# Folding the pooling's channel maps into the input projection of a two-layer decoder trunk

## The chip, the core and the metric

The kernel runs on one core of one Trainium2 chip. The metric is the device time of one execution in microseconds; the number given for a kernel is the median of its runs. The core has five engines, each with an instruction queue of its own that is worked off in order: TensorE (PE in the profile) multiplies matrices into PSUM; VectorE (DVE) and ScalarE (ACT) work element by element; GpSimd (POOL) does small things here; SyncE (SP) issues all the data transfers (DMA). Engines wait for one another through semaphores.

## What is computed

The input is 2048 tokens of 1024 channels. Two layers follow, each with a residual sum, and a last RMS norm. The change touches the first layer only. There one projection of the normalised tokens gives 512 pooled channels, 512 channels for a state-space model (SSM) and 1024 gate channels. The pooled channels lie in four groups of 128. Group g has a causal mean over the last 2, 4, 8 or 16 tokens, minus the token itself, and then a linear map of its own over its 128 channels:

```
proj = einsum('bsd,de->bse', h, w_in)
u_pool = proj[..., :512]
c = cumsum(u_pool, tokens)                       # per group g, window w
pooled_g = (c - c shifted by w) / min(pos, w) - u_pool_g
mixed_g = einsum('bsc,cd->bsd', pooled_g, pool_w[g])
y_pool = mixed * pool_scale
y = concat([y_pool, y_ssm]) * silu(z)
x = x + einsum('bse,ed->bsd', y, w_out)
```

Sums over tokens and maps over channels can be done in either order.

## The kernel before

**Precision.** Large products run on operands that are split in two parts of type fp32r, a rounded one (`hi`) and the rest (`lo`); a product is the sum of three: hi by hi, hi by lo, lo by hi. Small products (SSM, transposes, norms) run on plain fp32 operands.

**Streams and the planner.** The program is written as many streams (Python generators), each of which yields operations (`Op`), waits for a named event (`Wait`) and requests for buffers (`Alloc`). The class `Sched` merges them when the program is built. It keeps an estimated clock for each engine and a price for each operation, and takes as the next one the operation that can start soonest by these clocks; among those of one engine that can start within a small slack (`SLACK`: 0.02 for PE, 0.3 for SP), the stream of lower rank number goes first, and the stream `main` goes last. The result is one fixed order per engine; on the chip each engine keeps to it and waits where it must. So the prices matter only through the order. The price of a PE batch is in `mmb`:

```
d = sum(width(o) / 2400.0 if x.dtype == F32R else max(width(o), 128 if w.shape[1] > 64 else 0) / 600.0
        for o, w, x, s, e in batch) + 0.0027 * len(batch)
```

By it a fp32r product of 512 columns and a fp32 product of 128 columns have the same price: 0.2133 + 0.0027 = 0.216 us.

**Buffers.** Fixed pools of slots: `st` (8, general), `po` (2, results on their way to DRAM), `raw` (2, weights as loaded), `w` (8, split weights, two for each job), `act` (25), `pwt` (1), and in PSUM `mm` (3 of 1024 columns) and `aux` (2 of 512). A stream that finds no free slot stays behind until one is given back; an `Alloc` of two needs two free at once.

**The main stream** is the list of PE units in fixed order. A unit is one projection of 128 output channels: 8 blocks of input channels, each with 3 products for each block of 512 tokens, so 48 products of 512 columns for 1024 tokens. For the first half of the tokens (A) the order is: `A.s0` to `A.s2` on token block 0, then the same on block 1, `A.s3`, then `A.pu0`, `A.pz0`, `A.pu1`, `A.pz1` and so on to `A.pz3`, then `A.z0` to `A.z3`. `s` are SSM inputs, `pu` the pooled channels of a group, `pz` their gates. The second half (B) runs the same list, then the output projections, then layer 1.

**Weights.** Each unit has a `Job`. `fetch_thread` loads the jobs in their order into the two `raw` slots (512 KB each); `split_thread` makes hi (ACT) and lo (DVE) of them in two `w` slots, which are given back when the unit ends. While the SSM tables are being made, two of the eight `w` slots are taken by them.

**The start.** `norm_block` loads four x tiles of 128 tokens (four `st` slots), scales them (`norm_scale`, ACT, POOL), and once all four are scaled transposes them on PE in 8 steps, each through an `aux` slot to ACT and DVE (`norm_out`). It runs for block 0, then for block 1. The four `st` slots are given back after the last transpose. Beside it `ssm_prep` and what it starts load small tables (15 transfers) and compute the SSM tables, nearly all on DVE. `ssm_tables` makes four tables `ca` of six DVE operations each; for each, `ssm_w` has a batch of 16 small products on PE (the table batches below).

**Pooling.** `post_pool_u` brings the result of a `pu` unit to DRAM (`upd`). `pool_worker` then runs `pool_thread` for the four groups: it loads the tile, makes the window sums and subtracts the token (DVE), loads the group's map `pool_w` (64 KB, through an `st` slot), splits the map and the sums into hi and lo (ACT, DVE), loads the gate `z0d`, multiplies in one batch of six products of 512 columns into an `mm` slot, and scales and gates the result (DVE, from PSUM). The result goes to DRAM and is read much later by the output projection's `ypool_thread`.

Of the kernel before, what the change touches and what calls it, by code (L numbers as in the profile page):

```python
# [70 lines left out]
class Sched:  # L71
    """Merges several instruction streams into one program order. Each stream
    yields its operations; the estimated engine clocks decide which comes next."""
# [15 lines left out]
    def pool(self, name, n, make):  # L89
        """n slots; make(slot, dtype) gives a new tile in a slot."""  # L90
        self.pools[name] = list(range(n))
        self.make[name] = make
# [5 lines left out]
    def done(self, *key):  # L98
        self.keys.add(key)
# [57 lines left out]
    def advance(self, th, value=None):  # L157
        """Runs a stream up to its next operation; True if it got anywhere."""
        moved = False
        if th.block is not None:  # L160
            value = self.unblock(th.block)
            if value is None:
                return False
            th.block = None
            moved = True
        while True:
            try:
                y = th.gen.send(value)
            except StopIteration:
                self.threads.remove(th)  # L170
                return True
            moved = True
            value = None
            if isinstance(y, Op):
                y.ready = self.ready(y)
                th.op = y
                return True
            value = self.unblock(y)
            if value is None:
                th.block = y  # L180
                return True
# [50 lines left out]
def trunk(ctx, tc, io):  # L232
# [24 lines left out]
    slots("pwt", 1, 256)  # L257
# [24 lines left out]
    # ------------------------------------------------------------ operations  # L282
# [58 lines left out]
    def mmb(batch):  # L341
        """A batch of products (out, stationary, moving, start, stop)."""
        d = sum(width(o) / 2400.0 if x.dtype == F32R else max(width(o), 128 if w.shape[1] > 64 else 0) / 600.0
                for o, w, x, s, e in batch) + 0.0027 * len(batch)

        def emit():
            for o, w, x, s, e in batch:
                nc.tensor.matmul(o, w, x, start=s, stop=e)  # L348
        rd = []
        wr = []  # L350
        for o, w, x, s, e in batch:
            for l, ap in ((rd, w), (rd, x), (wr, o)):
                if not any(ap is y for y in l):
                    l.append(ap)
        op = Op("PE", d, rd, wr, emit)
        op.n = len(batch)
        return op
# [9 lines left out]
    # ------------------------------------------------------------ constants  # L367
# [36 lines left out]
    # ------------------------------------------------------------ DRAM scratch  # L404
# [9 lines left out]
    y1d = [[dram(f"y1d{b}_{kp}", (128, 1024)) for kp in range(4)] for b in range(2)]  # L414
    Ed = [dram(f"Ed{u}", (128, 1024)) for u in range(8)]
# [10 lines left out]
    # ------------------------------------------------------------ weights  # L426
    class Job:
        def __init__(self, srcs, name):
            self.srcs, self.name, self.pool = srcs, name, "w"
# [4 lines left out]
    def job_cols(w, c0, name):  # L434
        return Job([(lambda r: r.rearrange("p (k e) -> p k e", k=NK),
                     w[:, c0:c0 + 128].rearrange("(k p) e -> p k e", p=128))], name)

# [12 lines left out]
    def fetch_thread():  # L450
        for job in jobs:
            job.raw = yield Alloc("raw")
            for view, src in job.srcs:
                yield dma(view(job.raw), src)
            done("raw", job)
# [12 lines left out]
    # ------------------------------------------------------------ activations  # L468
    class Acts:
        """hi/lo parts of a [channels, 1024 tokens] operand: slots of two k by 512 tokens."""  # L470
# [46 lines left out]
    # ------------------------------------------------------------ rms norm  # L517
# [10 lines left out]
    def norm_block(src, keys, gname, acts, b, gate=None):  # L528
        """Normalises 512 tokens and puts them into acts, channels on partitions."""
        if gate:  # L530
            yield Wait(gate)
        xs = []
        for t in range(4):
            yield Wait(keys(b * 4 + t))
            if src is None:
                x = x1t.pop(keys(b * 4 + t)[1:])
            else:
                x = yield Alloc("st")
                yield dma(x[:, :1024], src(b * 4 + t))
            xs.append(x)  # L540
            boot = acts is h0[0] and b == 0
            spawn(norm_scale(xs[t][:, :1024], (acts.name, "n", b, t), boot), 1 if boot else 2, f"{acts.name}n{b}{t}")
        done("boot", acts.name, b)
        for t in range(4):
            yield Wait((acts.name, "n", b, t))
        yield Wait(("vcol",))
        for k in range(NK):
            if k % 2 == 0:
                yield from acts.alloc(k // 2, b)
            ps = yield Alloc("aux")  # L550
            yield trb([(ps[:, t * 128:(t + 1) * 128], xs[t][:, k * 128:(k + 1) * 128], ident) for t in range(4)])
            spawn(norm_out(ps, gname, acts, k, b), 1, f"{acts.name}o{k}{b}")
        free("st", *xs)
# [25 lines left out]
    # ------------------------------------------------------------ units of the tensor engine  # L579
# [10 lines left out]
    def etile_units(specs, acts, head, tail=0):  # L590
        """Projections; the first `head` run on block 0 alone while block 1 is still
        being normalised, the last `tail` so that block 0 makes room early."""
# [21 lines left out]
    # ---- layer 0 posts  # L614
# [36 lines left out]

    def pool_worker(h):
        for gi in range(4):
            yield Wait(("up", h, gi))
            yield from pool_thread(h, gi)

    def pool_thread(h, gi):
# [16 lines left out]
        if h == 0:  # L674
# [3 lines left out]
        w2 = yield Alloc("pwt", None, F32R)  # L678
        pr, = yield Alloc("st", 1)
        yield dma(pr[:, 0:128], io["pool_w"][0, gi])  # L680
        whi, wlo = w2[:, 0:128], w2[:, 128:256]
        yield acopy(whi, pr[:, 0:128])
        yield tt(wlo, pr[:, 0:128], whi, ALU.subtract)
        free("st", pr)
        hi_, lo_ = yield Alloc("st", 2, F32R)
        hi, lo = hi_[:, 0:H], lo_[:, 0:H]
        yield acopy(hi, s[:, 16:n])
        yield tt(lo, s[:, 16:n], hi, ALU.subtract)
        sz = s[:, 0:H]
        yield Wait(("zp", h, gi))  # L690
        yield dma(sz, z0d[h][gi])
        ps = yield Alloc("mm")
        yield mmb([(ps[:, b * 512:(b + 1) * 512], w, x[:, b * 512:(b + 1) * 512], i == 0, i == 2)
                   for i, (w, x) in enumerate(((whi, hi), (whi, lo), (wlo, hi))) for b in range(2)])
        free("st", hi_, lo_)
        free("pwt", w2)
        yield stt(sz, ps, vc("pool_scale", gi), sz, ALU.mult, ALU.mult)
        free("mm", ps)
        yield dma(y0d[h][gi], sz)
        free("st", s)  # L700
# [12 lines left out]
    # ------------------------------------------------------------ SSM tables  # L713
# [35 lines left out]
    def wrap(r, n, a):  # L749
        """r = a reduced to one turn."""  # L750
# [5 lines left out]
    def cmul_into(o_r, o_i, a_r, a_i, b_r, b_i, x, y, conj=False):  # L756
        """o = a b, or a times the conjugate of b."""
# [181 lines left out]
    def ssm_tables():  # L939
        """Per four pairs of groups: C times powers 1..8 of the rates, turns of the  # L940
        chunk rates, powers 0..7 of the rates times B."""
# [58 lines left out]
    def ssm_w(i, wt, ca):  # L1000
        """Products inside a chunk, and the way out of the states."""
# [53 lines left out]
    def ssm_first(z):  # L1055
        """SSM of the first half of the tokens, which also puts the tables into DRAM."""
# [26 lines left out]
    # ------------------------------------------------------------ SSM main  # L1083
# [75 lines left out]
    # ------------------------------------------------------------ layer 0 out  # L1159
# [149 lines left out]
    # ------------------------------------------------------------ layer 1  # L1309
# [19 lines left out]
    def conv_thread():  # L1329
        """Tap by tap; the last tiles block by block, all first blocks first."""  # L1330
# [21 lines left out]
    def pe_tables():  # L1352
        """Shifted copies of the taps for the convolutions on the tensor engine."""
# [12 lines left out]
    def pe_conv(n, j):  # L1366
        """Convolution of 128 channels as products: 8 channels by 16 phases of the
        tokens at a time, three neighbouring columns of 16 tokens."""
# [253 lines left out]
    # ------------------------------------------------------------ program  # L1622
# [6 lines left out]
    def l0_units(h):  # L1629
        p = P[h]  # L1630
        specs = [(f"{p}.s{q}", lambda q=q: job_cols(w_in0, 512 + q * 128, f"ws{h}{q}"), post_u(h, q)) for q in range(4)]
        for gi in range(4):
            specs.append((f"{p}.pu{gi}", lambda gi=gi: job_cols(w_in0, gi * 128, f"wpu{h}{gi}"), post_pool_u(h, gi)))
# [94 lines left out]
    spawn(norm_block(x_rows(0), lambda t: ("go",), "even_norm", h0[0], 1, (h0[0].name, "n", 0, 3)), 2, "n0A1")  # L1728
    for h in range(2):
# [20 lines left out]
    for n, j in enumerate(PEC):  # L1750
# [13 lines left out]
        "odd_norm", "odd_w_in", "conv_w", "conv_b", "conv_ln_g", "conv_ln_b", "odd_w_out", "final_norm"]  # L1764
# [17 lines left out]
```

## Time and profile before

| | |
|---|---|
| median of 3 runs | 1534.59 us (1533.71 to 1536.25) |
| the profiled execution, span | 1533.6 us |
| PE busy | 1493.4 us, 7087 matmuls |
| DVE busy | 1090.1 us |
| ACT busy | 549.5 us |
| POOL busy | 124.2 us |
| moved by DMA | 271.35 MB |

The span runs from the first to the last instruction of one execution that the hardware profiler recorded; the runs are timed without it, so the two need not be equal, and here they lie 1.0 us apart. An engine's busy time is the time in which at least one instruction of it was under way. PE pipelines its products: a single product is shown with some 0.4 us, while the next one starts about 0.23 us after it, so prices of products are read from the distance of starts.

### The profile page before, as it was taken

What the parts mean: (1) busy time and instruction counts of PE and PEld (TensorE: products, weight loads), DVE (VectorE), ACT (ScalarE), POOL (GpSimd) and SP (SyncE); (2) the same over time, 40 slices, a digit from 0 to 9 for tenths busy, and PEclk for the clock granted to TensorE, in tenths of its full rate; (3) what the DMA queues carried; (4) which work ended last, traced back from release to release, by engine and by line L of the source; (5) the groups of instructions that cost most, each with busy time, mean ns of one, the idle gap of its engine ahead of it and who ended that gap; (6) DMA issues with size and microseconds to landing.
All of it is one profiled execution on the core that took longest, in us unless ns stands there. A gap on an engine that the chain in (4) does not pass through costs nothing. (4 is left out here: it accounts for less than half of the span.)

```text
span 1533.6 us, 18686 instructions
## 1 busy us (share of the span) xinstructions
PE 1493.4 (97%) x7087; PEld 1224.7 (80%) x7087; DVE 1090.1 (71%) x1291; ACT 549.5 (36%) x859; POOL 124.2 (8%) x397
## 2 busy tenths in 40 slices
PE   5999999999999999999999999999999999999997
PEld 4878788888887788888888888888888888887785
DVE  5891567778857323399999999344997898967752
ACT  5322463222134215311111430352354565533431
POOL 4000121000000002000000000120000000003322
PEclk9999999999999999999999999999999999999999
DMA  6227973889665544233353543633466585966753
GB/s 193 83 86 234 313 238 116 255 266 332 221 222 194 168 165 137 83 97 95 98 97 112 191 144 118 218 98 111 88 148 202 160 248 188 354 217 226 246 200 115
DMA packets 248618, 271.35 MB, mean 177 GB/s; under 512 B 58497, under 2 KB 178993, under 8 KB 248528
## 3 DMA queue, kind: packets, MB, share of 16 engines
q1 hardware_dynamic: 248528, 270.15, 55.6%
q8 instruction: 56, 0.92, 0.2%
q14 instruction: 34, 0.28, 0.1%
HBM read 174.49 MB, written 91.42 MB: 173 GB/s over the span
## 5 line engine op out<-in xcount | busy, mean ns | idle before, releaser
L348 PE MATMUL mm<-act,w 128*128 128x512 f32 x4224 | 1004.9, 396 | 0.0
L348 PEld LDWEIGHTS mm<-act,w 128*128 128x128 f32 x4224 | 789.0, 189 | 178.2 <-issue 2.5
L305 DVE SCALAR_TENSOR_TENSOR ca<-cg,cwt,ca 128x1024 f32<-128x1024 f32 (+1 forms) x360 | 397.8, 1106 | 16.1 <-ACT ca L330 5.8
L348 PE MATMUL mm<-w,act 128*128 128x512 f32 x1344 | 316.6, 395 | 1.4 <-DVE w L287 1.4
L348 PEld LDWEIGHTS mm<-w,act 128*128 128x128 f32 x1344 | 251.7, 188 | 60.4 <-DVE w L287 1.8
L287 DVE TENSOR_TENSOR w<-raw,w 128x1024 fp32r<-128x1024 f32 x116 | 141.6, 1222 | 104.3 <-ACT w L319 101.8
L319 ACT CAST w<-raw 128x1024 fp32r<-128x1024 f32 x116 | 121.2, 1045 | 195.6 <-PE mm L348 152.1
L330 ACT ACTIVATE junk<-st 128x1024 bf16<-128x1024 f32 (+1 forms) x64 | 54.0, 844 | 121.3 <-DVE st L287 111.8
L305 DVE SCALAR_TENSOR_TENSOR act<-aux,vcol,act 128x512 fp32r<-128x512 f32 x64 | 45.9, 748 | 66.1 <-ACT act L330 66.0
L287 DVE TENSOR_TENSOR st<-st,mm 128x512 f32<-128x512 f32 x48 | 31.0, 684 | 74.7 <-PE mm L348 74.5
L330 ACT ACTIVATE po<-mm 128x1024 f32<-128x1024 f32 x32 | 32.9, 1027 | 119.8 <-PE mm L348 79.2
L319 ACT CAST act<-st 128x512 fp32r<-128x512 f32 (+1 forms) x64 | 51.8, 860 | 59.1 <-DMA st<-y0d 16.2
L297 POOL TENSOR_SCALAR sml<-sml 128x1 f32<-128x1 f32 (+1 forms) x100 | 34.4, 344 | 430.8 <-ACT junk L330 423.5
L319 ACT COPY st<-aux 128x512 f32<-128x512 f32 (+2 forms) x56 | 25.7, 474 | 114.9 <-PE aux L348 99.7
L330 ACT ACTIVATE act<-act,mask 128x128 f32<-128x128 f32 x192 | 58.0, 390 | 19.4 <-DMA act<-band 19.4
L521 POOL TENSOR_TENSOR sml<-sml,mhalf 128x1 f32<-128x1 f32 (+1 forms) x52 | 34.4, 662 | 346.2 <-DVE sml L295 342.2
L287 DVE TENSOR_TENSOR act<-st,act 128x512 fp32r<-128x512 f32 (+1 forms) x64 | 56.2, 926 | 8.3 <-ACT act L319 8.3
L330 ACT ACTIVATE act<-aux,vcol 128x512 fp32r<-128x512 f32 x64 | 41.6, 686 | 47.6 <-PE aux L362 47.5
L362 PE MATMUL aux<-ident,st 128*128 128x128 f32 (+2 forms) x266 | 38.9, 282 | 20.2 <-DMA st<-in_even_norm 8.7
L330 ACT ACTIVATE st<-mm 128x1024 f32<-128x1024 f32 x24 | 24.6, 1025 | 87.1 <-PE mm L348 84.5
L362 PEld LDWEIGHTS aux<-ident,st 128*128 128x128 f32 (+2 forms) x266 | 32.4, 146 | 28.3 <-POOL sml L297 8.7
L305 DVE SCALAR_TENSOR_TENSOR st<-st,mm 128x1024 f32<-128x1024 f32 x24 | 34.3, 1429 | 23.9 <-PE mm L348 23.9
(146 smaller groups left out, 1001.5 us busy)
## 6 DMA issues: line engine op xcount, KB each, us to landing
raw<-in_odd_w_in SPq DMA_DIRECT2D x48, 512.0 KB
raw<-in_even_w_in SPq DMA_DIRECT2D x32, 512.0 KB
st<-x1d SPq DMA_DIRECT2D x48, 256.0 KB
st<-in_x SPq DMA_DIRECT2D x16, 512.0 KB
raw<-in_even_w_out SPq DMA_DIRECT2D x16, 512.0 KB
z1d<-po SPq DMA_DIRECT2D x16, 512.0 KB
st<-z1d SPq DMA_DIRECT2D x16, 512.0 KB
raw<-in_odd_w_out SPq DMA_DIRECT2D x16, 512.0 KB
```

The lines of the kernel that those rows point to most:

```text
L287: return Op("V", d, [a, b], [o], lambda: V.tensor_tensor(o, a, b, op))
L297: e.tensor_scalar(o, a, s1, s2, op0, op1)
L305: return Op("V", d, rd, [o], lambda: V.scalar_tensor_tensor(o, a, s, b, op0, op1))
L319: return Op("A", 0.05 + width(o) / 960.0, [a], [o], lambda: A.copy(o, a))
L330: return Op("A", (0.3 if len(wr) > 1 else 0.13) + width(o) / 960.0, rd, wr, lambda: A.activation(o, a, fn, **kw))
L348: nc.tensor.matmul(o, w, x, start=s, stop=e)
L362: nc.tensor.transpose(o, a, idn)
L521: yield Op("G", 0.3, [a], [o], lambda: G.tensor_tensor(o, a, mhalf[:, :n], ALU.pow))
```

## The change

A new stream `pool_fold` multiplies each group's map into the 128 projection columns of that group, once: it loads the group's columns, transposed to channel by input (`pool_in`, a new input, which is the same weights in another layout), and the map, makes eight fp32 products of 128 columns in two batches, copies them out of PSUM and stores them to DRAM (`wpd`). The `pu` jobs of both halves load `wpd` in place of the columns of `w_in`, and wait for the group's fold. The projection then gives mapped channels; `pool_thread` sums them over tokens, and its own product, with the splits and the loads of the map before it, is gone. The stream starts when `main` reaches its first unit, which is at the start of the program. The `pwt` slot is half as wide. (The rest of the diff takes comment lines out.)

```diff
-    slots("pwt", 1, 256)
+    slots("pwt", 1, 128)
...
+    wpd = [dram(f"wpd{g}", (128, 1024)) for g in range(4)]
...
     class Job:
-        def __init__(self, srcs, name):
-            self.srcs, self.name, self.pool = srcs, name, "w"
+        def __init__(self, srcs, name, key=("go",)):
+            self.srcs, self.name, self.pool, self.key = srcs, name, "w", key
...
+    def job_fold(gi, name):
+        return Job([(lambda r: r[:, :1024], wpd[gi])], name, ("wp", gi))
...
     def fetch_thread():
         for job in jobs:
             job.raw = yield Alloc("raw")
+            yield Wait(job.key)
             for view, src in job.srcs:
                 yield dma(view(job.raw), src)
             done("raw", job)
...
+    def pool_fold():
+        yield Wait(("u", "A.s0.0"))
+        for gi in range(4):
+            wt, ot = yield Alloc("st", 2)
+            pw_ = yield Alloc("pwt")
+            yield dma(wt[:, :1024], io["pool_in"][gi])
+            yield dma(pw_, io["pool_w"][0, gi])
+            for q in range(2):
+                ps = yield Alloc("aux")
+                yield mmb([(ps[:, i * 128:(i + 1) * 128], wt[:, (4 * q + i) * 128:(4 * q + i + 1) * 128], pw_,
+                            True, True) for i in range(4)])
+                yield acopy(ot[:, q * 512:(q + 1) * 512], ps)
+                free("aux", ps)
+            free("pwt", pw_)
+            free("st", wt)
+            yield dma(wpd[gi], ot[:, :1024])
+            free("st", ot)
+            done("wp", gi)
...
         yield stt(s[:, 16:n], s[:, 16:n], 1.0 / win, u[:, 16:n], ALU.mult, ALU.subtract)
         free("st", u)
-        w2 = yield Alloc("pwt", None, F32R)
-        pr, = yield Alloc("st", 1)
-        yield dma(pr[:, 0:128], io["pool_w"][0, gi])
-        whi, wlo = w2[:, 0:128], w2[:, 128:256]
-        yield acopy(whi, pr[:, 0:128])
-        yield tt(wlo, pr[:, 0:128], whi, ALU.subtract)
-        free("st", pr)
-        hi_, lo_ = yield Alloc("st", 2, F32R)
-        hi, lo = hi_[:, 0:H], lo_[:, 0:H]
-        yield acopy(hi, s[:, 16:n])
-        yield tt(lo, s[:, 16:n], hi, ALU.subtract)
-        sz = s[:, 0:H]
+        zt = yield Alloc("st")
+        sz = zt[:, 0:H]
         yield Wait(("zp", h, gi))
         yield dma(sz, z0d[h][gi])
-        ps = yield Alloc("mm")
-        yield mmb([(ps[:, b * 512:(b + 1) * 512], w, x[:, b * 512:(b + 1) * 512], i == 0, i == 2)
-                   for i, (w, x) in enumerate(((whi, hi), (whi, lo), (wlo, hi))) for b in range(2)])
-        free("st", hi_, lo_)
-        free("pwt", w2)
-        yield stt(sz, ps, vc("pool_scale", gi), sz, ALU.mult, ALU.mult)
-        free("mm", ps)
+        yield stt(sz, s[:, 16:n], vc("pool_scale", gi), sz, ALU.mult, ALU.mult)
+        free("st", s)
         yield dma(y0d[h][gi], sz)
-        free("st", s)
+        free("st", zt)
         done("yp", h, gi)
...
-            specs.append((f"{p}.pu{gi}", lambda gi=gi: job_cols(w_in0, gi * 128, f"wpu{h}{gi}"), post_pool_u(h, gi)))
+            specs.append((f"{p}.pu{gi}", lambda gi=gi: job_fold(gi, f"wpu{h}{gi}"), post_pool_u(h, gi)))
...
+    spawn(pool_fold(), 3, "fold")
...
+        if name == "pool_in":
+            a = np.ascontiguousarray(np.asarray(inputs["even_w_in"])[0][:, :512].reshape(D, 4, 128).transpose(1, 2, 0))
```

More of the change, by code (lines that the diff above doesn't have):

```diff
@@ L1763 @@
         "ssm_b_re", "ssm_b_im", "ssm_c_re", "ssm_c_im", "ssm_d", "ssm_w_glu", "even_w_out",
-        "odd_norm", "odd_w_in", "conv_w", "conv_b", "conv_ln_g", "conv_ln_b", "odd_w_out", "final_norm"]
+        "odd_norm", "odd_w_in", "conv_w", "conv_b", "conv_ln_g", "conv_ln_b", "odd_w_out", "final_norm", "pool_in"]
 def kernel(**inputs):
@@ L1773 @@
     for name in _INS:
-        a = np.ascontiguousarray(inputs[name])
+        if name == "pool_in":
+            a = np.ascontiguousarray(np.asarray(inputs["even_w_in"])[0][:, :512].reshape(D, 4, 128).transpose(1, 2, 0))
+        else:
+            a = np.ascontiguousarray(inputs[name])
         arrays[f"in_{name}"] = a
```

## The prediction, made before the changed kernel was run

> **What bounds the kernel now.** I read the page's busy shares first, then its forty slices.
>
> ```profile
> span 1533.6 us, 18686 instructions
> PE 1493.4 (97%) x7087; PEld 1224.7 (80%) x7087; DVE 1090.1 (71%) x1291; ACT 549.5 (36%) x859; POOL 124.2 (8%) x397
> ...
> PE   5999999999999999999999999999999999999997
> ```
>
> PE is busy in nearly every slice; DVE is next, with 71%. Next the view of waits, for PE alone and from 20 us on:
>
> ```profile
> PE aux L348 <- DMA act<-ud: 2.5, 3, 1.8
> PE aux L362 <- DMA st<-in_conv_w: 2.3, 1, 2.3
> ...
> PE aux L348 <- DVE act L287: 2.0, 2, 1.9
> ...
> PE aux L348 <- DMA st<-Gd: 0.3, 1, 0.3
> ```
>
> All its ten rows come to some 15 us, the longest single wait being 2.3 us. So PE's own work sets the time, and a product taken off PE is worth its start-to-start distance, if nothing else turns up late in its place. The profiled span is 1533.6 us, the median 1534.6; I add what I find to the median.
>
> **What goes.** Eight pool batches of six products leave PE (two halves by four groups).
>
> ```profile
> 181.87 1.55 PE L348 MATMUL mm<-st,pwt 128*128 128x512 f32 x6
> 183.25 1.05 PE L348 MATMUL aux<-act,st 128*128 128x128 f32 x8
> 184.06 11.38 PE L348 MATMUL mm<-act,w 128*128 128x512 f32 x48
> ...
> 436.55 1.64 PE L348 MATMUL mm<-st,pwt 128*128 128x512 f32 x6
> 438.02 26.44 PE L348 MATMUL mm<-act,w 128*128 128x512 f32 x114
> 464.31 0.61 PE L348 MATMUL mm<-st,pwt 128*128 128x512 f32 x2
> 466.29 1.20 PE L348 MATMUL mm<-st,pwt 128*128 128x512 f32 x4 [1.37 <-DVE st L287]
> 467.33 34.95 PE L348 MATMUL mm<-act,w 128*128 128x512 f32 x150
> ```
>
> From the first batch's start to the next instruction's are 1.38 us (181.87 to 183.25), at 436.55 it is 1.47. I take 1.42: 8 x 1.42 = 11.4 us. The batch at 464.31 also waits 1.37 us for its own split on DVE. That wait goes, and what stands behind it, the products at 467.33, shows no wait of its own: 1.4 us more. Together **12.8 us**. What else goes is off PE: per group a split of 1024 columns on ACT and DVE each, a small split, and a 64 KB load. The last DVE step stays, reading SBUF in place of PSUM. It all lies beside PE and counts nothing; so does the slot relief (one `st` slot for two, no `mm` slot), whose results are not read before the output projections.
>
> **What comes.** The fold adds 4 x 8 = 32 fp32 products of 128 columns. The nearest row has the same form: eight such from 183.25 to 184.06, 0.81 us, 0.10 each. By it 32 cost **3.3 us** of PE. The Trainium skill, in FP8 and Floating Point Precision, section TensorE Precision Notes, says a true fp32 product takes four passes through the array; by that, 128 columns would cost as much as 512 at full rate, and the fold about 7.4 us. The row, with 0.10 us against 0.23 for 512 columns, disagrees; I take the row.
>
> ACT copies eight results of 512 columns out of PSUM, and SP issues 12 transfers (4 x 512 KB and 4 x 64 KB in, 4 x 512 KB out):
>
> ```profile
> L319 ACT COPY st<-aux 128x512 f32<-128x512 f32 x28 | 16.5, 589 | 68.6 <-PE aux L348 64.7 <-issue 3.9
> ...
> 41.00:73.00 32.00, 32.00 (x156) 25.82 (x154) 27.85 (x75) 12.49 (x18) 0.00 (x0) 1.00 0.30 99
> ...
> 31.35 0.40 SPq L339 DMA_DIRECT2D raw<-in_even_w_in  x1
> 53.15 0.35 SPq L339 DMA_DIRECT2D ud<-po  x1
> ...
> 58.61 1.05 ACT L319 CAST w<-raw 128x1024 fp32r<-128x1024 f32 x1
> ```
>
> 8 x 0.589 = 4.7 us of ACT fall where ACT is busy 12.5 of 32 us; the DMA engines are busy 0.30 there, and SP issues nothing between 31.4 and 53.2 us. That is the cover. The transfer at 31.35 is `pu0`'s weights; it will wait for the first fold and be some microseconds late, with the `ud` stores and later weights queued behind it on SP. But its split, the fifth of the `w` casts, is made only at 58.6, when `s1` gives its slots back, and `pu0` starts later still, behind `s3`. Without that cover each microsecond would be one of PE. Cost: 0.
>
> **The order is the real price.** The planner's formula prices a fold product at 0.216 us, the same as a product of 512 columns, though the chip does it in 0.10. Every fold product that it places ahead of some event therefore pushes one product of `main` behind that event. And around 77 to 90 us there is such an event, set by DVE:
>
> ```profile
> 77.33 0.69 DVE L287 TENSOR_TENSOR act<-cg 128x512 f32<-128x512 f32 x1
> ...
> 80.77 1.22 DVE L287 TENSOR_TENSOR w<-raw,w 128x1024 fp32r<-128x1024 f32 x1
> ...
> 83.93 0.69 DVE L287 TENSOR_TENSOR act<-cg 128x512 f32<-128x512 f32 x1
> ...
> 89.47 0.69 DVE L287 TENSOR_TENSOR act<-cg 128x512 f32<-128x512 f32 x1
> ...
> 77.63 0.30 PE L348 MATMUL aux<-ca,cg 128*32 128x16 f32 x4
> ...
> 84.67 0.37 PE L348 MATMUL aux<-act,cg 128*32 128x112 f32 x1 [0.15 <-DVE act L287]
> ...
> 90.21 0.37 PE L348 MATMUL aux<-act,cg 128*32 128x112 f32 x1 [1.89 <-DVE act L287]
> ...
> 60.00:80.00 20.00, 20.00 (x136) 15.44 (x135) 19.56 (x31) 5.87 (x10) 0.00 (x0) 1.00 0.37 124
> ```
>
> The last three table batches start when DVE's tables end: 78.02, 84.62 and 90.16. DVE is busy 19.6 of 20 us before that, with nothing of the fold in it. So PE is at 90.2 us whatever it did earlier. If all four folds lie ahead of that point, 32 products of `main` fall behind it, and cost 32 x 0.2306 (438.02 to 464.31: 26.29 us for 114) = 7.4 us, not 3.3: PE merely waits longer at the first table batch, by about 7.4 - 3.3 = 4.1 us. From the 7.4 goes up to 1.2 us, if the weight split at 80.77, whose slots come free when `s3` ends, now falls behind the tables: I take 0.6. Cost of the fold: **6.8 us** (3.3 to 7.4).
>
> **The start.** `main` reaches its first unit at once, so the fold takes two of the eight `st` slots at time zero. Block 0's rows hold four, so block 1's third and fourth row tiles find none, and load only after block 0's last transposes.
>
> ```profile
> 0.72 1.82 SPq L339 DMA_DIRECT2D st<-in_x  x4
> ...
> 4.43 1.06 ACT L330 ACTIVATE junk<-st 128x1024 bf16<-128x1024 f32 x1 [2.44 <-DMA st<-in_x]
> ...
> 19.13 1.05 SPq L339 DMA_DIRECT2D st<-in_x  x2
> ...
> 27.64 0.66 PE L362 MATMUL aux<-ident,st 128*128 128x128 f32 x4 [0.20 <-DVE act L305]
> ...
> 33.71 1.06 ACT L330 ACTIVATE junk<-st 128x1024 bf16<-128x1024 f32 x1
> ...
> 38.54 1.15 ACT L330 ACTIVATE st<-st,sml 128x1024 f32<-128x1024 f32 x1 [1.58 <-POOL sml L285]
> ...
> 40.58 1.04 PE L362 MATMUL aux<-ident,st 128*128 128x128 f32 x8
> ```
>
> They are issued about 28.4 in place of 19.1 us. But the fourth is squared only at 33.7, as ACT has other work before it, without idle time. The program's first tile took 3.7 us from issue (0.72) to use (4.43), so by an estimate the fourth is there at about 33. Little is lost; POOL and ACT lead from there to the transposes at 40.58, which had about 0.9 us in hand (scaled at 39.69). Bounds: 0 and the full 9.4 less 0.9 = 8.5 us; I take the near end, **0.5 us**.
>
> **Sum.** -12.8 + 6.8 + 0.5 = -5.5 us: 1534.6 - 5.5 = **1529.1 us**. What follows PE's last product does not change.
>
> **Rivals.**
> *The plain sum* (faster). If the planner's PE has holes before 73 us that the fold fills, or most folds land behind the tables, the fold costs only 3.3: -12.8 + 3.3 = -9.5, 1525.1 us. For it: PE is full from 20 us on in the trace. Against it: the three batches tied to DVE's ends.
> *Four passes.* If a fold product takes as long as one of 512 columns, 0.2306 us, the fold is 7.4 us of PE work that fills the wait at the tables: -12.8 + 7.4 + 0.5 = -4.9, 1529.7 us. That is the page's rule above; the row speaks against it.
> *New waits.* Every order after the fold is made anew. A wait costs more than itself:
>
> ```profile
> 73.00:92.00 19.00, 16.96 (x167) 1.00 0.16 56
> 92.00:110.00 18.00, 18.00 (x76) 0.91 0.27 90
> ```
>
> After 1.9 us of waiting the granted clock is 0.91 for 18 us, 1.6 us lost. The Trainium skill, TensorE: Matmul & The Clock Gate, Part 1: The HAM clock gate, lets the clock drop only after an idle window of about 3.4 us; by it shorter waits would cost only themselves. The row has a drop after less, so I count the loss. Two new waits of some 1 to 2 us, with 1.6 each, cost 5 to 7 us and eat the gain: about 1534.
> *The row tiles* (slower). Block 1's late rows show in full: 8.5 in place of 0.5 gives 1537.1. It decides as soon as the fourth row's square starts more than about 6 us later than 33.7. For it: slots are taken for sure. Against it: the landing time above.
> *A starved fold* (slower). The fourth fold may not get its two slots before the SSM stage holds them all:
>
> ```profile
> 114.26 1.22 DVE L305 SCALAR_TENSOR_TENSOR st<-st,st 128x1024 f32<-128x1024 f32 x1
> ...
> 164.79 0.81 SPq L339 DMA_DIRECT2D st<-in_pool_w  x1
> 155.07 1.03 ACT L330 ACTIVATE po<-mm 128x1024 f32<-128x1024 f32 x1
> ```
>
> The first pool stream is done with its sums at 115.5 and can load its map only at 164.8: it waits 50 us for one slot. A fold that falls into this has its weights some 15 us after 165 (load 4, products and copies 2, store 3, load 4, split 2), while `pu3` is due at about 155, where `pz2`'s result is read: 25 us lost, 1534.6 - 9.5 + 25 = 1550. Against it: four folds in series at 10 us each end near 70 us.
>
> **Chances and range.** 1529.1 by the DVE-bound order 0.44, with its own range 1526.5 to 1531.5; the plain sum 0.22; four passes 0.04; new waits, no change to speak of, 0.16; row tiles 0.09; starved fold 0.05. A measurement of this kernel can tell about 0.2%, 3.1 us, so "same" is 1531.5 to 1537.7. The row tiles in part (1537.1 lies at the edge) I count half as same, half as slower; some of the new waits may add up to more than the gain. Faster 0.70, same 0.18, slower 0.12. The range takes in the plain sum with some 3 us below it for waits that go with the new order, and new waits above: 1522 to 1536.
>
> **What would show it.** PE's matmuls fall by 16 (48 go, 32 come). The fold's eight-product groups take 0.8 us, not 1.9. The four folds lie ahead of the table batches, and PE's wait for DVE's `act` tables grows from 2.0 to some 5 us, with fewer products of `main` ahead of 90 us; in the plain sum that wait stays at 2. Block 1's first transposes stay near 41 us. No PE wait falls to the `wpd` loads. I am wrong if those tables end at another time, if a wait for `raw` or `wpd` appears, or if PE's other waits from 20 us on grow by more than 4 us.

## The result

| | before | after |
|---|---|---|
| median | 1535.42 us (4 runs, 1533.71 to 1537.45) | 1551.45 us (4 runs, 1550.65 to 1554.43) |
| ratio to before, 95% interval | 1 | 1.0097 [1.0076, 1.0119] |
| span of the profiled execution | 1533.6 us | 1552.7 us |

The changed kernel is slower by some 16 us, where 5.5 us faster was forecast. The head of its page (PEclk is the clock that the throttle granted to PE, in tenths of full speed):

```profile
span 1552.7 us, 18699 instructions
PE 1493.0 (96%) x7103; PEld 1224.2 (79%) x7103; DVE 1078.8 (69%) x1275; ACT 544.1 (35%) x851; POOL 127.0 (8%) x397
...
PE   5999995999999999999999999999999999999997
...
PEclk9999997999999999999999999999999999999999
```

PE's busy time is what it was (1493.0 against 1493.4 us), and the span is 19.1 us longer: the time went into waiting. That the busy times agree so well is chance: some of PE's work is gone, and some of the rest ran at a low clock, as is seen below. The loss shows in one place, the seventh of the forty slices (about 233 to 272 us), where PE is half idle and its clock low. Two more things are in these lines. PE has 7103 matmuls, 16 more than before and not 16 fewer. And the fold stands in the list of waits, for its first weight:

```profile
PE aux L362 <- ACT st L330: 17.7, 1, 17.7
...
PE aux L348 <- DMA pwt<-in_pool_w: 6.1, 2, 5.6
PE aux L348 <- DMA act<-ud: 3.6, 2, 2.2
...
PE aux L348 <- DVE act L287: 1.0, 2, 0.5
```

The first row was 1.0 us before: now it is one wait of 17.7 us for ACT's scaling (L330) of an x row tile (`st`), ahead of the transposes of L362. The 5.6 us of the second row lie ahead of 14.6 us, where PE has little else to do. The table batches' wait for DVE, for which growth to some 5 us was forecast, has the last row: 1.0 us.

The long wait in the timeline of the changed kernel (start, duration, engine, line, operation, and in brackets the idle time before it with its releaser), all engines, followed backwards from the transposes:

```profile
245.91 0.49 PE L362 MATMUL aux<-ident,st 128*128 128x128 f32 x3
264.12 1.33 PE L362 MATMUL aux<-ident,st 128*128 128x128 f32 x5 [17.72 <-ACT st L330]
...
262.92 1.15 ACT L330 ACTIVATE st<-st,sml 128x1024 f32<-128x1024 f32 x1 [5.05 <-POOL sml L285]
...
256.72 1.06 ACT L330 ACTIVATE junk<-st 128x1024 bf16<-128x1024 f32 x1 [1.61 <-DMA st<-in_x]
...
252.03 0.33 SPq L339 DMA_DIRECT2D st<-in_x  x1
...
250.73 1.24 DVE L287 TENSOR_TENSOR st<-st 128x1037 f32<-128x1037 f32 x1 [1.22 <-DMA yd<-st]
```

Three of a block's four row tiles are there at 245.91, and PE transposes them. The fourth is loaded only at 252.03, right behind a step of a pool stream's window sums (250.73), whose end gives back an `st` slot. Then come 4.7 us to the square, 6.2 us to the scaling (POOL's small operations lie between) and 1.2 us to PE. So the row tile was late because it had no slot.

The view of windows shows what that cost (length, busy time of PE, PEld, DVE, ACT and POOL, granted clock, DMA share, GB/s). Before:

```profile
200.00:260.00 60.00, 59.04 (x323) 49.71 (x322) 41.35 (x60) 28.90 (x44) 11.80 (x29) 1.00 0.56 172
260.00:400.00 140.00, 139.28 (x721) 117.14 (x720) 112.05 (x163) 37.60 (x57) 3.33 (x13) 1.00 0.84 273
```

After:

```profile
200.00:260.00 60.00, 44.18 (x218) 36.80 (x216) 37.93 (x53) 20.09 (x26) 10.45 (x27) 0.88 0.83 259
260.00:400.00 140.00, 133.78 (x699) 111.87 (x700) 102.15 (x152) 42.72 (x66) 11.69 (x29) 0.96 0.64 211
...
225.00:246.00 21.00, 20.81 (x104) 17.79 (x105) 13.26 (x20) 6.88 (x8) 2.79 (x7) 0.92 0.53 165
...
264.00:268.00 4.00, 3.17 (x12) 2.58 (x13) 1.53 (x3) 2.12 (x4) 0.00 (x0) 0.50 0.66 173
268.00:272.00 4.00, 4.00 (x21) 3.39 (x20) 1.90 (x3) 1.80 (x4) 0.00 (x0) 0.76 0.54 191
272.00:280.00 8.00, 7.09 (x46) 5.51 (x46) 3.67 (x5) 5.79 (x12) 1.74 (x8) 1.00 0.38 122
```

Between 200 and 400 us PE is idle for 22.0 us (200 - 44.18 - 133.78), before for 1.7: 20.4 us more. The slow clock, counted where PE works, adds 1.7 us (0.08 of 21 us, behind a wait of 2.2 us) and 2.5 us (0.50 of 3.2 and 0.24 of 4, behind the long one). That is some 25 us lost; the 16 us of the result are this less what the change gains elsewhere.

**Who had the slot.** Of the streams that want `st` slots here, one is not in the front part: `ssm_g(1)` takes two for the second pair of SSM tables (`gt`) and keeps them long. Its work is plain in the trace, as two copies of 256 columns out of PSUM. ACT's timeline before, with the squares (`junk`) of the second half's eight row tiles, of which the first and the last are shown:

```profile
183.43 1.06 ACT L330 ACTIVATE junk<-st 128x1024 bf16<-128x1024 f32 x1 [5.10 <-DMA st<-in_x]
...
225.23 0.65 ACT L319 COPY st<-aux 128x256 f32<-128x256 f32 x2 [0.71 <-PE aux L362]
225.76 1.07 ACT L330 ACTIVATE junk<-st 128x1024 bf16<-128x1024 f32 x1
```

After:

```profile
184.07 0.65 ACT L319 COPY st<-aux 128x256 f32<-128x256 f32 x2 [9.70 <-PE aux L362]
...
186.44 1.07 ACT L330 ACTIVATE junk<-st 128x1024 bf16<-128x1024 f32 x1
...
278.43 1.07 ACT L330 ACTIVATE junk<-st 128x1024 bf16<-128x1024 f32 x1
```

Before, the pair is made at 225, behind seven of the eight row tiles. After, it is made at 184, ahead of all of them, and the last tile is squared at 278. **Theory A**: the fold puts `main` behind against the SSM streams; the gate of the second half's norm (`A.z0`, a unit of `main`) opens too late to be ahead of `ssm_g(1)`; the pair takes two slots, the norm's two blocks share what is left, and PE waits. Its rivals: **B**, that the fold's own work and the lateness of the main products cost the time, and the order of the slots only goes with them; **C**, that the fold's transfers hold up the x rows.

### The profile page after: what moved, and what is told of

Read it like the earlier page. It is cut to its first block, busy times and chain, and to the rows that moved or that the text cites. A ratio compares the mean times of both kernels' runs of the same rounds, so it can differ in the third digit from the quotient of the medians.

```text
span 1552.7 us, 18699 instructions
## 1 busy us (share of the span) xinstructions
PE 1493.0 (96%) x7103; PEld 1224.2 (79%) x7103; DVE 1078.8 (69%) x1275; ACT 544.1 (35%) x851; POOL 127.0 (8%) x397
## 5 line engine op out<-in xcount | busy, mean ns | idle before, releaser
L305 DVE SCALAR_TENSOR_TENSOR ca<-cg,cwt,ca 128x1024 f32<-128x1024 f32 (+1 forms) x360 | 397.8, 1106 | 14.6 <-ACT ca L330 4.3
L330 ACT ACTIVATE junk<-st 128x1024 bf16<-128x1024 f32 (+1 forms) x64 | 54.0, 844 | 123.0 <-DVE st L287 92.3
L330 ACT ACTIVATE po<-mm 128x1024 f32<-128x1024 f32 x32 | 32.9, 1027 | 135.1 <-PE mm L348 68.1
L362 PE MATMUL aux<-ident,st 128*128 128x128 f32 (+2 forms) x266 | 39.7, 284 | 31.5 <-ACT st L330 17.7
L319 ACT COPY st<-aux 128x512 f32<-128x512 f32 (+2 forms) x64 | 30.3, 487 | 103.1 <-PE aux L348 82.8
L330 ACT ACTIVATE act<-act,mask 128x128 f32<-128x128 f32 x192 | 57.9, 390 | 18.8 <-DMA act<-band 18.7
L362 PEld LDWEIGHTS aux<-ident,st 128*128 128x128 f32 (+2 forms) x266 | 32.5, 147 | 40.6 <-ACT st L330 18.0
L330 ACT ACTIVATE act<-aux,vcol 128x512 fp32r<-128x512 f32 x64 | 41.9, 685 | 44.7 <-PE aux L362 44.6
L330 ACT ACTIVATE st<-mm 128x1024 f32<-128x1024 f32 x24 | 24.6, 1025 | 90.7 <-PE mm L348 88.7
```

Source lines behind the costliest of these rows:

```text
L305: return Op("V", d, rd, [o], lambda: V.scalar_tensor_tensor(o, a, s, b, op0, op1))
L319: return Op("A", 0.05 + width(o) / 960.0, [a], [o], lambda: A.copy(o, a))
L330: return Op("A", (0.3 if len(wr) > 1 else 0.13) + width(o) / 960.0, rd, wr, lambda: A.activation(o, a, fn, **kw))
L362: nc.tensor.transpose(o, a, idn)
```

## The experiments

All ratios are to the kernel before on the same chip, whose medians were 1537.84, 1537.02, 1536.83 and 1538.17 us in the four sets below.

**Norm first.** The changed kernel; the pair waits until the first of the norm's two blocks has taken its four slots.

```diff
     def ssm_g(i, wb_s, wb):
+        if i == 1:
+            yield Wait(("boot", h0[1].name, 0))
         gt = yield Alloc("st", 2)
```

> The changed kernel, with one line more: the SSM stream of the second table group waits, before it asks for its pair of st slots, until the norm of the second half's block 0 has its four. Theory A (the loss is an order of slots: the fold delays the main stream by some 7 us, so that this pair is taken ahead of the norm, whose fourth row tile then comes late, and PE waits 17.7 us and runs at a lower clock behind it): the 17.7 us wait is gone and the time is 1527 to 1531, by 1535.4 - 12.8 (the pool products and their wait) + 6.5 (64 fp32 matmuls of 0.10 us). Theory B (the fold itself, with its slots and transfers, is what costs): stays within 4 us of 1551.

Measured: 1529.38 us, 0.9943 [0.9926, 0.9959]. In its timeline of ACT the pair is back behind six of the eight row tiles, and in its windows PE is full:

```profile
223.39 0.65 ACT L319 COPY st<-aux 128x256 f32<-128x256 f32 x2 [0.40 <-PE aux L362]
...
231.47 1.04 ACT L330 ACTIVATE junk<-st 128x1024 bf16<-128x1024 f32 x1
```

```profile
200.00:260.00 60.00, 58.06 (x313) 48.53 (x312) 40.13 (x57) 31.89 (x48) 13.86 (x36) 1.00 0.62 195
260.00:400.00 140.00, 140.00 (x738) 118.95 (x737) 107.63 (x160) 34.27 (x54) 7.27 (x13) 1.00 0.81 269
```

One line about slots, with the whole fold still there, takes some 24 us off by the ratios (1.0097 to 0.9943; 22 us by the two medians, which come from different sets of runs). Neither B nor C allows that.

**Gate early.** The same by another way: the norm's gate moves two units up the list of `main`.

```diff
-GATE_B = 'A.z0'
+GATE_B = 'A.pu3'
```

> The changed kernel, with the norm of the second half let go two units earlier (at A.pu3 in place of A.z0, some 23 us earlier), and no other edit. Theory A: the norm asks for its slots before the second pair of the SSM tables does, so the long wait is gone as in the run before, 1526 to 1532. Theory B: no gain, 1547 to 1555.

Measured: 1528.96 us, 0.9939 [0.9922, 0.9955]; the pair is made at 232.5, and the long wait is gone.

**No fold.** The changed kernel without the fold, with nothing done about the order. The `pu` jobs load plain columns, and the channel maps are left out of the computation.

```diff
-            specs.append((f"{p}.pu{gi}", lambda gi=gi: job_fold(gi, f"wpu{h}{gi}"), post_pool_u(h, gi)))
+            specs.append((f"{p}.pu{gi}", lambda gi=gi: job_cols(w_in0, gi * 128, f"wpu{h}{gi}"), post_pool_u(h, gi)))
...
-    spawn(pool_fold(), 3, "fold")
```

> The changed kernel without the fold: its stream is not started, and the pu jobs load the plain projection columns, so the channel maps are left out of what is computed. What is left of the change is the removal of the pool products, their splits and loads, and the other use of slots in the pool stream. Theory A: main is not delayed, no long wait at the second half's norm; 1535.4 - 12.8 = 1522.6, between 1520 and 1526. Rival C (the pool stream's new use of slots makes the norm starve): the long wait stays, 1540 or more.

(The rival C of this expectation is another than the C above: it is the pool stream's new use of slots.)

Measured: 1524.05 us, 0.9904 [0.9887, 0.992]; the pair is made at 219.2, and PE waits 4.3 us at most between 180 and 300 us, for an SSM load. So it is the fold that turns the order over, not the removal of the pool products. Against norm first, the fold with its order mended costs 5.3 us. Against before, the removal is worth 13.8 us, though in an order that is made anew too.

**Before, delayed.** The kernel before with eight batches of four fp32 products that nobody uses, started at unit `A.s1`, to put `main` late without a fold.

```diff
+    def pe_delay():
+        yield Wait(("u", "A.s1.0"))
+        for n in range(8):
+            ps = yield Alloc("aux")
+            yield mmb([(ps[:, i * 128:(i + 1) * 128], ident, ident, True, True) for i in range(4)])
+            yield Op("V", 0.15, [ps], [mask8], lambda p=ps: V.tensor_copy(mask8[:, 0:1], p[:, 0:1]))
+            free("aux", ps)
...
+    spawn(pe_delay(), 3, "delay")
```

> The kernel before, with 32 products on PE that nobody needs, of the fold's size (fp32, 128 columns, eight batches of four, through aux, each emptied by one small DVE copy), from the second unit on; no st slot and no transfer is added, and the pooling is as before. Theory A: the delay of the main stream alone turns the order of the slots; the second half's norm starves, PE waits some 15 to 20 us at its transposes, and the time is 1553 to 1562. Theory B (slots and transfers of the fold): 1535.4 + 6.5 = 1542, no long wait.

Measured: 1560.11 us, 1.0138 [1.0112, 1.0164]. The time is that of theory A, and the pair is made early, at 187.9. But as a test it is weak. Seven of the eight batches fell behind 114 us (still ahead of the gate), and the table batches themselves moved, which isn't what the delay was meant to do. PE's timeline:

```profile
112.81 0.27 PE L348 MATMUL aux<-ca,cg 128*32 128x16 f32 x4 [3.29 <-DVE act L308]
...
114.90 2.08 PE L348 MATMUL aux<-ident 128*128 128x128 f32 x8 [0.54 <-DVE mask L1719]
...
222.34 2.05 PE L348 MATMUL aux<-act,st 128*128 128x128 f32 x8 [5.52 <-DMA act<-ud]
```

The lost time lies in several waits of 2.8 to 5.5 us rather than in one. That called for a cleaner test.

**Pair first.** The kernel before, with no fold and no work added; the norm's two blocks may take slots only when the pair has its two.

```diff
         gt = yield Alloc("st", 2)
+        if i == 1:
+            done("pair")
...
-                spawn(norm_block(x_rows(1), lambda t: ("go",), "even_norm", h0[1], b, ("u", GATE_B)), 2, f"n0B{b}")
+                spawn(after(("pair",), norm_block(x_rows(1), lambda t: ("go",), "even_norm", h0[1], b, ("u", GATE_B))), 2, f"n0B{b}")
```

> The kernel before, with no fold in it, whose second-half norm may take its st slots only once the second table pair (ssm_g of i = 1) has taken its own two; nothing else is changed and no work is added. Theory A (the changed kernel is slow through that order of the st slots alone): about 22 us over the kernel before, the distance of the changed kernel (1551.5) from the same kernel with the order put back (1529.4), so 1553 to 1560; TensorE waits over 10 us once between 240 and 270 us for a row tile's square on ScalarE, and its clock falls below 0.9 in the stretch behind. Theory B (the lateness of the main products is what costs, and the order only goes with it): nothing is late here, so within 4 us of the kernel before. Rival C (the fold's loads and stores hold up the x rows on the queue): there is no fold traffic here, so no change either.

Measured: 1553.16 us, 1.0107 [1.0084, 1.0129]: as slow as the changed kernel, in a kernel that has nothing of the change. That the two agree so closely is chance: the order alone costs 16 us here, and in the changed kernel the 24 us that norm first gives back. Its PE timeline and a window:

```profile
239.83 0.80 PE L348 MATMUL aux<-act,act 128*128 128x128 f32 x2 [5.65 <-DVE act L287]
248.91 1.33 PE L362 MATMUL aux<-ident,st 128*128 128x128 f32 x5 [5.08 <-ACT st L330]
```

```profile
200.00:260.00 60.00, 48.04 (x235) 39.56 (x234) 37.48 (x55) 22.78 (x32) 9.19 (x27) 0.89 0.78 241
```

The size came out at the low end of what was written down (16.1 us over before; 1553 to 1560 us had been given, with 22 us as the centre), and so did the clock under 0.9. The single wait of over 10 us didn't: it is split in two of 5 to 6 us, and PE is idle 12.0 us in the window. The order brings the loss; how large it is and where in the queue it surfaces differ from program to program.

**Late fold, alone and with the line.** The fold starts when the first half's second block is normalised.

```diff
-        yield Wait(("u", "A.s0.0"))
+        yield Wait((h0[0].name, 7, 1))
```

With the line of norm first:

> The changed kernel with the order put back (the line of the run norm first) and the fold started only when the second block of the first half is normalised, near 60 us, in place of the first ws weight's products. Without any fold the time was 1524.1, with it and the order put back 1529.4. If those 5.3 us are the fold's own 64 matmul instructions of 0.10 us (6.5 us of TensorE in the chain), the start makes no difference: 1528 to 1531. If they are what the fold does to the start (a first batch at 2.08 us, a wait of 5.5 us for its weight, both ahead of 20 us) they go: 1524 to 1527.

Measured: 1533.54 us, 0.9979 [0.9966, 0.9992], outside both expectations. The fold's early start is not what it costs; starting it later costs more. Why was not followed up.

With the gate at `A.pz3` in place of the line:

> The late fold again, but in place of the line in ssm_g the second half's norm opens one projection tile group earlier (gate at A.pz3 for A.z0). Theory A: either way the norm takes its st slots ahead of the pair, so the same time as the late fold with the line, within 2 us, and no TensorE wait over 4 us between 180 and 300 us. Were the earlier gate itself a gain, 3 us or more below that run; were it no cure, above 1545.

Measured: 1530.56 us, 0.996 [0.9947, 0.9973]; the pair is made at 229.8, and the one PE wait between 180 and 300 us is 0.5 us. The cure works by the gate too. The run stands 3 us below the one with the line, which had been written down as the sign of a gate that gains by itself, though the two intervals overlap.

Without any cure:

> The changed kernel with the fold started only when the second block of the first half is normalised, and nothing done about the order of the st slots. Theory A: by the end of the table products near 90 us the main products are as far behind as in the changed kernel, since the fold's 6.5 us lie ahead of it either way; so the pair still goes first, TensorE still waits over 10 us between 240 and 280 us, and the time is 1545 to 1565. If the disturbed start (the first 40 us) were what shifted the order, the norm gets its slots as before and the time is 1524 to 1530.

Measured: 1569.07 us, 1.0207 [1.019, 1.0223]. The pair comes first again, and the price is higher still, above the range given. The single wait of over 10 us didn't come: the longest is 8.2 us, for an SSM load. ACT's timeline and a window:

```profile
188.27 0.65 ACT L319 COPY st<-aux 128x256 f32<-128x256 f32 x2 [14.14 <-PE aux L362]
...
297.33 1.06 ACT L330 ACTIVATE junk<-st 128x1024 bf16<-128x1024 f32 x1
```

```profile
260.00:400.00 140.00, 112.75 (x570) 94.79 (x569) 100.55 (x151) 34.81 (x53) 8.20 (x25) 0.89 0.67 224
```

The last row tile is squared at 297 here, and PE is idle 27 of 140 us. By 92 us this kernel has begun more main products than the changed one (206 against 194), by 200 us about as many (612 against 618), and it still loses more: against B.

**Fold twice.** Norm first, with each batch of the fold issued twice into the same bank.

```diff
-                            True, True) for i in range(4)])
+                            True, True) for i in range(4)] * 2)
```

> The changed kernel with the order put back, and each of the fold's eight batches of four fp32 products issued twice into the same bank (32 more products of 128 columns, same result). It measures the disputed price: at 0.20 us a product (two instructions of 0.10 each) 6.5 us more than the run norm first, 1534.5 to 1537.5; at the 0.10 of the prediction 3.3 us more, 1531.5 to 1533.5. Both hold only while the order of the st slots stays put, so no TensorE wait over 4 us between 180 and 300 us.

Measured: 1531.56 us, 0.996 [0.994, 0.9981], so 0.0017 or 2.6 us above norm first, with a span of 1529.6 against 1526.4 us. PE's groups that read `pwt`, in the view of lines, here and in norm first:

```profile
L348 PE MATMUL aux<-pwt,st x128: 270/275/579, 14.5 to 68.1; 128*128 128x128 f32 x128
```

```profile
L348 PE MATMUL aux<-pwt,st x64: 272/275/579, 14.6 to 63.6; 128*128 128x128 f32 x64
```

Thirty-two more products are 64 more instructions, and PE's busy time grows from 1487.5 to 1493.4 us: 5.9 us, 0.18 each. So a product takes 0.2 us of PE, but less than half of it reaches the end: by its time alone the run falls into the range given for 0.10, and it is the count of instructions and PE's busy time that speak for 0.20. The 2.6 us themselves lie within the intervals. And `main` is later still (168 main products begun by 92 us, 196 in norm first), while nothing worse than those 2.6 us happens, as the order is held. That is the plainest evidence against B.

**The cures without the change.** The kernel before with the gate moved, as a control, and the changed kernel with the same gate.

> A control: the kernel before with the gate of the second half's norm at A.pz3 for A.z0. In the kernel before the norm has its slots ahead of the pair already, so theory A expects no change: within 3 us of the kernel before. If the earlier gate gives time by itself (x rows of the second half loaded sooner), 4 to 8 us below it, and the gains of the two repaired versions over the kernel before would not be the change's own.

> The changed kernel with the gate of the second half's norm at A.pz3 for A.z0 and nothing else, to be set beside the kernel before with the same gate, which was at 0.9955 of the kernel before. Theory A: this gate also lets the norm take its st slots ahead of the pair, so no TensorE wait over 10 us between 240 and 280 us, and 0.990 to 0.997 of the kernel before. If the change itself is worth the prediction's 5.5 us once the order is out of the way, it stands at or below 0.992; if it is worth about nothing under one and the same gate, at 0.994 to 0.997.

> The second such pair: the kernel before with the gate at A.pu3, to be set beside the changed kernel with that gate, which was at 0.9939 of the kernel before. If the change itself is worth 5.5 us under one and the same gate, this stands at 0.996 to 0.999; if it is worth about nothing, at 0.993 to 0.995. Theory A expects no TensorE wait over 4 us between 180 and 300 us in it.

| gate of the second half's norm | before's code | changed code |
|---|---|---|
| `A.pz3` | 1530.1 us, 0.9955 [0.9942, 0.9969] | 1529.37 us, 0.9943 [0.9924, 0.9961] |
| `A.pu3` | 1530.31 us, 0.9951 [0.9933, 0.9968] | 1528.96 us, 0.9939 [0.9922, 0.9955] |

The control missed its expectation: before, too, gains some 7 us by the earlier gate, although its order of pair and norm was right already. So the gain of the cured versions over before is mostly not the change's. Under one and the same gate the change is worth 0.0012, 1.8 us, twice; each interval alone is wider than that, so it can't be told from nothing, and both runs lie nearer to what was written down for a change worth nothing than for one worth 5.5 us. What the gate saves before was not settled. The clock differs, but not with the gate. Between 500 and 560 us it is 0.97 before and 1.00 in before's code with either earlier gate (1.8 us), but 0.97 again in the changed code with either, which is no slower. Between 92 and 110 us it is 0.91 before (1.6 us lost), and in before's code at `A.pz3` and at `A.pu3`:

```profile
92.00:110.00 18.00, 18.00 (x81) 14.54 (x80) 16.97 (x47) 6.09 (x10) 0.00 (x0) 1.00 0.25 90
...
92.00:110.00 18.00, 18.00 (x76) 14.64 (x75) 16.95 (x46) 5.04 (x6) 0.00 (x0) 0.92 0.27 90
```

PE's wait for DVE just ahead of this window is the same in all three, 1.89, 1.85 and 1.84 us.

**All programs together.** When the pair is made, and when the last row tile of the second half is squared, by the profile of each:

| pair | last square | ratio | |
|---|---|---|---|
| 184.1 | 278.4 | 1.0097 | changed |
| 186.9 | 264.3 | 1.0107 | pair first |
| 187.9 | 275.8 | 1.0138 | before, delayed |
| 188.3 | 297.3 | 1.0207 | late fold alone |
| 219 to 233 | 223 to 236 | 0.9904 to 1 | before, and the nine others |

No program lies between. This, with norm first (the order put back, the loss goes) and pair first (the order alone, the loss comes), is what the verdict rests on. That the fold turns the order over is shown by no fold; that it does so by making `main` late can be read in PE's queue, whose order is the planner's. Ahead of `A.z0` stand 12 units of 48 products, so the gate opens behind 576 main products. The pair's first transposes on PE, before and after:

```profile
224.59 0.60 PE L362 MATMUL aux<-ident,act 128*128 128x128 f32 x4
...
183.41 0.63 PE L362 MATMUL aux<-ident,act 128*128 128x128 f32 x4 [0.94 <-DVE st L287]
```

Ahead of them stand 732 main products before and 693 in no fold: the gate was open. In the changed kernel there are 558, in the run *before, delayed* 546 and in *late fold alone* 570: it was still shut. At 183.4 us before has begun 588 main products and no fold 581, and these three 558, 534 and 556. So where nothing forced the order, the pair came first in just those programs in which `main` was late at the gate. The planner's own clocks were not read out.

## Why the prediction was wrong

**What bounds the kernel**: right. The loss is PE waiting, and a lower clock behind the waits. That PE's busy time is the same to 0.4 us does not say that its work is: with the order put back it is 1487.5 us.

**What goes**, 12.8 us: about right in kind, and not measured cleanly; no fold against before gives 13.8, but before has an order of its own that the gate shows to be worth 7.

**What comes**: a row was misread. The groups of eight at 183.25 are four products, each of two instructions. The changed kernel's own fold shows it:

```profile
40.21 1.06 PE L348 MATMUL aux<-pwt,st 128*128 128x128 f32 x8
41.02 1.64 PE L348 MATMUL mm<-act,w 128*128 128x512 f32 x6
```

This is one batch of four products, 0.81 us from start to start, 0.20 a product: 6.5 us for the 32, not 3.3. PE's matmuls go up by 64 and down by 48, which are the 16 more on the page. The rule of the Trainium skill that the prediction set aside (FP8 and Floating Point Precision, TensorE Precision Notes: a true fp32 product makes four passes) was nearly right: 7.4 us by it, an estimate. As the fold was already priced at 6.8 us for its effect on the order, the sum would hardly have moved, to the four-pass rival's 1529.7.

**The order is the real price**: this is the step that failed, though what it looked at came nearly as forecast. The last table batch of the changed kernel begins where DVE's tables allow, if 1.5 us earlier than before (88.73 against 90.21), and `main` is behind:

```profile
88.73 0.37 PE L348 MATMUL aux<-act,cg 128*32 128x112 f32 x1 [0.50 <-DVE act L287]
```

By 92 us 194 main products have begun, before 224: 30 fewer, forecast were 32. PE's wait did not grow to 5 us, as the fold's products fill twice the time that was thought. But the step priced the 32 late products as so much PE time and stopped at the table batches. It did not ask what else goes by `main`'s position: the gate `A.z0`, at which the second half's norm applies for slots, against streams that do not go by `main`. There the 17.7 us and the slow clock arose, some 25 us in all between 200 and 400 us, and no term of the sum stood for them. Of the signs of being wrong that were written down two came: the tables end at another time, and PE's other waits grow by more than 4 us.

**The start**, 0.5 us: right in that no more is lost. Block 1's first transposes start at 39.77, before at 40.58, so 0.8 us earlier.

**The rivals.** *New waits* had the right kind, a wait and a slower clock behind it, but priced it at two waits of 1 to 2 us. Its 1.6 us of lost clock for one such wait were read from one execution, and the same wait does not always bring them: the rows above have 0.92 and 1.00 behind it, and no fold has 1.00 behind 1.87 us. *A starved fold* had the right resource, `st` slots held by the SSM stage, and by luck nearly the right time (1550), but the wrong victim: the fold got its slots, the second half's row tiles did not. *Row tiles* asked the same question of the first half only. With the order put back the changed kernel is at 0.9943 of before, 8.8 us faster; under equal gates it is 1.8 us faster, within the noise. The forecast of 5.5 lies between the two, which bears out neither its terms nor its sum.

## What to carry to other kernels

In a program whose order is worked out by a planner, a few microseconds of new work cost first what they weigh and then what they turn over: list the gates that hang on the delayed stream, and for each the streams that compete for the same slots at that point. A change and its kernel before should be compared under more than one such gate before a gain is put down to the change; here the gate alone was worth more than the change. When a price is read off a group of rows, check its count against the code's loop, as one product need not be one instruction.

## What was not expected of the hardware

An fp32 product of 128 columns is two matmul instructions of about 0.10 us from start to start. Beside it, at the start of the program, the same batch of eight instructions took 1.87 us (14.58 to 16.45), against 0.81 us later. The profile gives a granted clock of 1.00 for 14.50 to 16.50 us too, so the clock on record does not explain it, and the cause is open.

```profile
14.58 2.08 PE L348 MATMUL aux<-pwt,st 128*128 128x128 f32 x8 [5.58 <-DMA pwt<-in_pool_w]
16.45 0.85 PE L362 MATMUL aux<-ident,st 128*128 128x128 f32 x3
```

After the 17.7 us wait PE worked at a granted clock of 0.50 for 4 us and at 0.76 for the next four, then at 1.00. The Trainium skill (TensorE: Matmul & The Clock Gate, Part 1: The HAM clock gate) names two states, half and full clock, and full after some 3.4 us of steady work; the trace agrees with half and full. By the means of the two stretches the change lies near 270 us (1.9 of the second 4 us at half), 5.8 us after work began, later than the Trainium skill has it; a further wait of 0.7 us lies between.
